# Differential attention with its probability–value products held back two blocks, six probability tiles instead of four, and GpSimd's ring of DMA descriptors at half its size

## The chip, the core and the metric

One core of one Trainium2 chip runs the whole program. The metric is the device time of one execution in microseconds (us), as the median of several; the kernel before takes 2479.04 us. Six actors are spoken of: TensorE (PE: matmuls and transposes; PEld is its weight load), VectorE (DVE), ScalarE (ACT), GpSimd (POOL, used here almost only to issue DMAs), SyncE (SP, which issues the weight loads), and the DMA engines. Each engine works through its own list of instructions in the order in which it stands, and waits where an instruction's input or buffer is not ready yet; whatever stands behind waits with it.

## What is computed

Two layers, each with three parallel token mixers (retention, differential attention, latent attention), gates, projections and a SwiGLU block, on 128 context tokens and 512 latent tokens (640 in all, five blocks of 128). Only differential attention is changed:

```python
def _diff_attention(q, k, v, lam, lam_init):
    s = jnp.einsum('bqhcd,bkhcd->bhcqk', q, k).astype(jnp.float32) * DIFF_HD ** -0.5
    p = jax.nn.softmax(s, axis=-1)
    a = p[:, :, 0] - lam * p[:, :, 1]
    o = jnp.einsum('bhqk,bkhe->bqhe', a.astype(v.dtype), v)
    return (_head_rmsnorm(o) * (1.0 - lam_init)).astype(v.dtype)
```

There are four heads; each query has two score maps (c = 0, 1), whose softmaxes are combined into one map `a` before the product with the values. Latent queries (blocks 1 to 4) see 640 keys, context queries (block 0) see 128.

## The kernel before

`diff` runs once per layer. It builds the keys, queries and values of head 0, then for each head first builds the next head (`build(hd + 1)`) and then calls `diff_head`. `diff_head` goes over the blocks in the order 1, 2, 3, 4, 0. Per block it makes, for c = 0 and 1, the scores (L836, L837, into the PSUM tile `S`, of which there are two), the maximum (L459), the exponential with its sum (L461, into an SBUF tile `dp`) and the reciprocal; the two maps are then combined in place on DVE (L850). Such a tile `dp` is taken from a group of four buffers (`bufs=4`, tag `p`).

The second half of a block, `diff_av`, is not done at once but handed to `later`, which keeps one stage back: the stage handed in before is carried out, the new one is stored. `diff_av` transposes the combined map on PE (L862, one instruction per 128 keys), ACT copies the result into `at` (L863; the one buffer of its tag), PE multiplies it with the values (L866, PSUM tile `O`, one buffer), ACT scales it into `osb` (L867) and takes the sum of squares, which writes into `at` again (L868). After the five blocks `diff_end` (also handed to `later`) makes the reciprocal root on DVE (`rsqrt`, L150 to L158, small operations in a row), scales `osb` (L875) and transposes it on PE (L880).

Between the blocks stands `self.fill()`: it takes work from a queue that `plan` laid out for this stage, 16 pieces of `gates` and 20 of `ret_values`. Both are groups of 24 matmuls each (L133) into the PSUM tile `G`, which has one buffer while filling: a gate group is emptied by ACT (L1024), a value group by ACT alone (L816) or by ACT and then DVE (L818, L819). In what follows these are called fill groups. What is left in the queue is done at the end of the stage (`flush`).

That is the order in which the program is written. The order in which each engine's list stands is set by the tile framework, which schedules the written instructions at build time; with the buffers of tag `p` it hands a free one to whichever map is next. So the written order is a priority rather than the order itself, and a number of buffers shows in it.

Retention (`ret`) follows; it needs nothing of differential attention but the memory that it leaves. On the host nothing is changed.

Of the kernel before, what the change touches and what calls it, by code (L numbers as in the profile page):

```python
# [12 lines left out]
F32 = mybir.dt.float32  # L13
# [8 lines left out]
P = 128  # L22
# [3 lines left out]
T = 640  # L26
# [24 lines left out]
class Kern:  # L51
    def __init__(self, ctx, nc, tc, io):
        self.nc, self.tc, self.io, self.ctx = nc, tc, io, ctx
        self.pe, self.act, self.dve, self.pool = nc.tensor, nc.scalar, nc.vector, nc.gpsimd

        self.pin = False
        self.gi, self.filling, self.fillers, self.pend = 0, False, [], None
        self.mod, self.ss = {}, {}
        self.const = self.sb("const", 1)
        self.hp = self.sb("hp", 1)  # L60
        self.ht = [self.hp.tile([P, KT, T], F32R, name=f"h{p}") for p in ("hi", "lo")]
        self.w = self.sb("w", 4)
        self.sm = self.sb("sm", 3)
        self.ps = ctx.enter_context(tc.tile_pool(name="ps", bufs=1, space=PSUM))
        self.dr = ctx.enter_context(tc.tile_pool(name="dr", bufs=1, space=DRAM))
# [20 lines left out]
        return self.ps.tile([P, 512], F32, tag="O", name="O", bufs=1)  # L86


    def later(self, stage):
        if self.pend is not None:  # L90
            self.pend()
        self.pend = stage


    def plan(self, points, *gens):
# [610 lines left out]
    def diff(self, l, act, yhi, ylo, ctx):  # L706
# [22 lines left out]
        def build(hd):  # L729
# [40 lines left out]
            for b0, nb in ((0, 1), (1, 2), (3, 2)):  # L770
# [9 lines left out]
                a.copy(q[:, :, 128 * b0:128 * (b0 + nb)], t.rearrange("p (c n) -> p c n", c=2)[:, :, 0:128 * nb])  # L780

        build(0)
        for hd in range(4):
            if hd < 3:
                build(hd + 1)
            self.diff_head(pool, Q[hd], K1[hd], K2[hd], V[hd], nlam, lam_init, yhi[:, hd, :], ylo[:, hd, :])
# [36 lines left out]
    def diff_head(self, pool, Q, K1, K2, V, nlam, lam_init, yhi, ylo):  # L823
        d, a, pe = self.dve, self.act, self.pe
        osb = pool.tile([P, NB, 128], F32, tag="osb", name="osb", bufs=1)
        ssq = self.sm.tile([P, NB], F32, tag="dssq", name="dssq", bufs=2)
        for b in (1, 2, 3, 4, 0):
            q0 = 128 * b
            w, nk, kb0 = (T, 5, 1) if b else (128, 1, 0)
            ps, zs = [], []  # L830
            zt = self.sm.tile([P, 8], F32, tag="dz", name="dz", bufs=4)
            for c in range(2):
                S = self.S()
                for j in range(2 if b else 1):
                    o, k0, n = (S[:, j, 0:320], 128 + 320 * j, 320) if b else (S[:, 0, 0:128], 0, 128)
                    pe.matmul(o, Q[:, c, q0:q0 + 128], K1[:, c, k0:k0 + n], start=True, stop=False)  # L836
                    pe.matmul(o, Q[:, c, q0:q0 + 128], K2[:, c, k0:k0 + n], start=False, stop=True)  # L837
                p = pool.tile([P, T], F32, tag="p", name="dp", bufs=4)
                z, tot = zt[:, c:c + 1], zt[:, c + 2:c + 3]
                if b:  # L840
                    self.softmax(S[:, :, 0:320], p.rearrange("p (a n) -> p a n", a=2), z, 0.125, tot)
                else:
                    self.softmax(S[:, 0, 0:128], p[:, :128], z, 0.125, tot)
                ps.append(p)
                zs.append((z, tot))

            r = zt[:, 4:5]
            d.scalar_tensor_tensor(r, zs[1][0], nlam, zs[0][1], op0=ALU.mult, op1=ALU.mult)
            aw = ps[0]
            d.scalar_tensor_tensor(aw[:, :w], ps[1][:, :w], r, ps[0][:, :w], op0=ALU.mult, op1=ALU.add)  # L850
            self.fill()
            self.later(lambda *x, b=b, w=w, nk=nk, kb0=kb0, aw=aw, z0=zs[0][0]: self.diff_av(pool, b, nk, kb0, aw, z0, V, osb, ssq))
        self.later(lambda: self.diff_end(pool, osb, ssq, lam_init, yhi, ylo))

    def diff_av(self, pool, b, nk, kb0, aw, z0, V, osb, ssq):
        d, a, pe = self.dve, self.act, self.pe
# [683 lines left out]


def build(arrays):
    nc = bacc.Bacc("TRN2", target_bir_lowering=False, num_devices=1)
    io = {}
    for name, a in arrays.items():
        io[name] = nc.dram_tensor(name, a.shape, mybir.dt.from_np(a.dtype), kind="ExternalInput").ap()
    for name, shape in OUTS.items():
        io[name] = nc.dram_tensor(name, shape, F32, kind="ExternalOutput").ap()
    with tile.TileContext(nc, schedule_with_timeline_sim=True) as tc, ExitStack() as ctx:
        Kern(ctx, nc, tc, io).run()  # L1550
    return nc
# [16 lines left out]
```

## Time and profile before

| | |
|---|---|
| median of three runs | 2479.04 us (2477.76 to 2480.05) |
| the profiled execution | 2480.35 us, its span on the core 2478.1 us |
| PE busy | 2399.8 us, 97% of the span |
| PEld, DVE, ACT, POOL busy | 2337.6, 1710.0, 1054.5, 155.0 us |
| DMA | 248.99 MB, mean 100 GB/s |

Read it so: PE is busy nearly all the time, and its amount of work is fixed by the program; the span is PE's work and PE's idle time. The instructions of PE overlap in the pipeline, so an instruction's duration (0.27 to 0.31 us for most) is longer than the distance to the next one. The two differential stages lie at about 320 to 494 us (layer 0) and 1549 to 1729 us (layer 1).

### The profile page before, as it was taken

The numbers are of one execution on the slowest core, as the hardware profiler recorded it, in microseconds if no ns is written. First come the engines' busy times: TensorE is split into PE (matmuls) and PEld (weight loads), VectorE is DVE, ScalarE is ACT, GpSimd is POOL, SyncE is SP. The second block draws the span as 40 slices with busy tenths as digits, with TensorE's granted clock in tenths as the row PEclk, the third lists the DMA queues.
The fourth block names the chain that finished last, engine by engine and source line by source line (L and its number), as shares of the span: only waits on it lengthen the run. The fifth ranks groups of instructions, "written<-read, shape, count | busy, mean of one in ns | idle before, by whom it ended". The sixth has DMA issues, their size and how long they took to land.

```text
span 2478.1 us, 43132 instructions
## 1 busy us (share of the span) xinstructions
PE 2399.8 (97%) x17008; PEld 2337.6 (94%) x17008; DVE 1710.0 (69%) x3835; ACT 1054.5 (43%) x2209; POOL 155.0 (6%) x266
## 2 busy tenths in 40 slices
PE   8999999999999999999999999999999999999997
PEld 5999998999999999999989999989999999999996
DVE  5767676566788766656677776765663478777776
ACT  5655565522234322222275664655322354333344
POOL 0000210000000000000000002100000000000001
PEclk9999999999999999999999999999999999999998
DMA  6211221332554444444342123213213212222222
GB/s 263 69 67 60 94 85 55 108 98 69 190 168 128 149 136 149 136 132 139 103 135 69 60 69 99 76 57 111 85 60 116 76 57 90 73 81 90 69 77 69
DMA packets 81435, 248.99 MB, mean 100 GB/s; under 512 B 10608, under 2 KB 20048, under 8 KB 80336
## 3 DMA queue, kind: packets, MB, share of 16 engines
q1 hardware_dynamic: 53856, 164.13, 20.4%
q0 software_dynamic: 21328, 76.12, 9.5%
q10 hardware_dynamic: 6048, 5.98, 0.7%
q8 instruction: 134, 2.20, 0.4%
q14 instruction: 69, 0.57, 0.1%
HBM read 225.97 MB, written 20.22 MB: 99 GB/s over the span
## 4 chain that ended last, share of the span: by engine, by line
PE 86%; DVE 7%; ACT 3%; issue 3%; DMA 1%; POOL 0%; DVEq 0%; ACTq 0%; POOLq 0%
PE G L133 35%; PE S L133 23%; PE S L1116 4%; PE S L1115 4%; PE S L1114 4%; PE Tp L133 4%; PE O L866 1%; PE Tp L669 1%; PE O L644 1%; PE O L643 1%; DVE wlo L120 1%; PE S L836 1%; PE G L217 1%; DMA rq<-dproj 1%; PE Tp L360 1%
## 5 line engine op out<-in xcount | busy, mean ns | idle before, releaser
L117 ACT CAST whi<-raw 128x1024 fp32r<-128x1024 f32 (+4 forms) x346 | 301.9, 880 | 584.3 <-PE G L133 222.3
L120 DVE TENSOR_TENSOR wlo<-raw,whi 128x1024 fp32r<-128x1024 f32 (+4 forms) x346 | 348.9, 1011 | 199.8 <-ACT whi L117 198.7
L133 PE MATMUL G<-whi,hhi 128*128 128x256 f32 x1040 | 299.1, 288 | 6.9 <-DVE rvs L819 3.9
L133 PE MATMUL G<-whi,hlo 128*128 128x256 f32 x1040 | 295.4, 284 | 0.0
L133 PE MATMUL G<-wlo,hhi 128*128 128x256 f32 x1040 | 294.4, 283 | 0.0
L1116 PE MATMUL S<-hhi,wlo 128*128 128x320 f32 x736 | 226.4, 310 | 2.6 <-DVE wlo L120 2.6
L1115 PE MATMUL S<-hlo,whi 128*128 128x320 f32 x736 | 227.5, 310 | 0.2 <-DVE hlo L120 0.2
L1114 PE MATMUL S<-hhi,whi 128*128 128x320 f32 x736 | 226.7, 309 | 0.0
L133 PE MATMUL G<-ghi,whi 128*128 128x320 f32 x704 | 220.3, 313 | 5.3 <-DVE x L1076 4.0
L133 PE MATMUL G<-glo,whi 128*128 128x320 f32 x704 | 217.4, 309 | 0.0
L133 PE MATMUL G<-ghi,wlo 128*128 128x320 f32 x704 | 217.4, 309 | 0.0
L133 PEld LDWEIGHTS G<-whi,hhi 128*128 128x128 f32 x1040 | 198.0, 191 | 10.5 <-DVE rvs L819 5.2
L133 PEld LDWEIGHTS G<-wlo,hhi 128*128 128x128 f32 x1040 | 198.4, 191 | 0.0
L133 PEld LDWEIGHTS G<-whi,hlo 128*128 128x128 f32 x1040 | 198.3, 191 | 0.0
L248 DVE SCALAR_TENSOR_TENSOR junk<-rawr,csr 128x1024 bf16<-128x1024 f32 x160 | 195.2, 1220 | 1.2
L1076 DVE SCALAR_TENSOR_TENSOR x<-G,mod,x 128x128 f32<-128x128 f32 (+2 forms) x336 | 136.3, 435 | 81.1 <-PE G L133 80.7
L133 PE MATMUL S<-hhi,whi 128*128 128x320 f32 x588 | 184.1, 313 | 2.9 <-DVE gt L1043 2.7
L133 PE MATMUL S<-hhi,wlo 128*128 128x320 f32 x588 | 181.9, 309 | 0.0
L133 PE MATMUL S<-hlo,whi 128*128 128x320 f32 x588 | 181.8, 309 | 0.0
L133 PE MATMUL G<-hhi,whi 128*128 128x320 f32 x512 | 161.7, 316 | 7.6 <-ACT gt L1024 4.7
L133 PE MATMUL G<-hlo,whi 128*128 128x320 f32 x512 | 159.1, 311 | 0.0
L133 PE MATMUL G<-hhi,wlo 128*128 128x320 f32 x512 | 158.7, 310 | 0.0
(438 smaller groups left out, 6268.6 us busy)
## 6 DMA issues: line engine op xcount, KB each, us to landing
raw<-w_ffn_in SPq DMA_DIRECT2D x88, 512.0 KB, 3.7
rawr<-w_adat POOLq DMA_DIRECT2D x80, 512.0 KB, 3.9
raw<-w_gate SPq DMA_DIRECT2D x48, 512.0 KB, 3.3
raw<-w_ffn_out SPq DMA_DIRECT2D x64, 256.0 KB, 2.7
raw<-w_diff SPq DMA_DIRECT2D x24, 512.0 KB, 3.5
raw<-w_branch SPq DMA_DIRECT2D x24, 512.0 KB, 3.6
raw<-w_ret SPq DMA_DIRECT2D x24, 512.0 KB, 3.4
raw<-w_ada SPq DMA_DIRECT2D x16, 512.0 KB, 9.7
```

Of the source, the lines that this page charges most:

```text
L117: (eng or self.act).copy(hi, src)
L120: (eng or self.dve).tensor_tensor(lo, src, hi.bitcast(F32), op=ALU.subtract)
L133: ins = self.pe.matmul(*args, **kw)
L217: self.pe.matmul(ps[32 * g:32 * g + 32, :], self.cs[:, k, :], raw[:, kk, :], start=k < 4, stop=k >= 4, tile_position=(0, 32 * g))
L248: self.tc.keep_in_program_order(d.scalar_tensor_tensor(junk, raw, 1.0, self.csr[:, i, :], op0=ALU.mult, op1=ALU.mult, accum_out=mod[:, n, ...
L360: self.pe.matmul(ps[:, :n], self.ones, sq[:, :n], start=k == 0, stop=k == KT - 1)
L643: self.pe.matmul(o[:, :n], vv, hi, start=i == 0, stop=False)
L644: self.pe.matmul(o[:, :n], vv, lo, start=False, stop=i == m - 1)
L1076: self.dve.scalar_tensor_tensor(x[h][:, n, c0:c1], ps[:, c0:c1], g[:, n, gi:gi + 1], x[h][:, n, c0:c1], op0=ALU.mult, op1=ALU.add)
L1114: self.pe.matmul(o, lh, rh, start=k == 0, stop=False)
L1115: self.pe.matmul(o, lh, rl, start=False, stop=False)
L1116: self.pe.matmul(o, ll, rh, start=False, stop=k == nk - 1)
```

## The change

`later` becomes a list: it carries out the oldest stage once more than `depth` stages are waiting. `diff_head` hands in its stages with depth 2; the latent attention calls it as before, with depth 1. The maps get six buffers. To make room, the part of each partition of SBUF that holds GpSimd's ring of DMA descriptors is set to 8192 bytes, half of the framework's default; a map tile takes 2560 bytes of a partition.

```diff
-        self.gi, self.filling, self.fillers, self.pend = 0, False, [], None
+        self.gi, self.filling, self.fillers, self.pend = 0, False, [], []
...
-    def later(self, stage):
-        if self.pend is not None:
-            self.pend()
-        self.pend = stage
+    def later(self, stage, depth=1):
+        if stage is not None:
+            self.pend.append(stage)
+        while len(self.pend) > (0 if stage is None else depth):
+            self.pend.pop(0)()
...
-                p = pool.tile([P, T], F32, tag="p", name="dp", bufs=4)
+                p = pool.tile([P, T], F32, tag="p", name="dp", bufs=6)
...
-            self.later(lambda *x, b=b, w=w, nk=nk, kb0=kb0, aw=aw, z0=zs[0][0]: self.diff_av(pool, b, nk, kb0, aw, z0, V, osb, ssq))
-        self.later(lambda: self.diff_end(pool, osb, ssq, lam_init, yhi, ylo))
+            self.later(lambda *x, b=b, w=w, nk=nk, kb0=kb0, aw=aw, z0=zs[0][0]: self.diff_av(pool, b, nk, kb0, aw, z0, V, osb, ssq), 2)
+        self.later(lambda: self.diff_end(pool, osb, ssq, lam_init, yhi, ylo), 2)
...
-    nc = bacc.Bacc("TRN2", target_bir_lowering=False, num_devices=1)
+    nc = bacc.Bacc("TRN2", target_bir_lowering=False, num_devices=1, dynamic_dma_scratch_size=8192)
```

No instruction is added or removed. What moves are places in the lists of PE, DVE, ACT and (a little) POOL, within the two differential stages and, by a few rows, at the boundary between the layers. The new `later` is one line longer, so a line after it has a number that is higher by one in the changed kernel.

**The end of layer 0's stage, PE.** These are the rows of the last head from the products of block 2 on. `O` is the product of a block, `Tp` the transposes of the next block's map `dp`, and `G_5989` is a fill group of 24 matmuls, of which the first row stands here. Before:

```order
L866 MATMUL O_5886<-V_4915,at_5876 128x128 x4
L862 MATMUL Tp_6019<-ct_76,dp_5801 128x128 x4
L866 MATMUL O_5886<-V_4915,at_5876 128x128
L862 MATMUL Tp_6025<-ct_76,dp_5801 128x128
L133 MATMUL G_5989<-whi_5921,hhi_61 128x256
...
L866 MATMUL O_6028<-V_4915,at_6018 128x128 x4
L862 MATMUL Tp_6116<-ct_76,dp_5900 128x128
L866 MATMUL O_6028<-V_4915,at_6018 128x128
L862 MATMUL Tp_6116<-ct_76,dp_5900 128x128 x3
L862 MATMUL Tp_6122<-ct_76,dp_5900 128x128
```

Of the change, the same place (block 2 is `O_6010`, block 3 `O_6107`, block 4 `O_6125`, block 0 `O_6137`):

```order
L867 MATMUL O_6010<-V_4907,at_6000 128x128 x4
L863 MATMUL Tp_6098<-ct_76,dp_5783 128x128 x4
L867 MATMUL O_6010<-V_4907,at_6000 128x128
L863 MATMUL Tp_6104<-ct_76,dp_5783 128x128
L867 MATMUL O_6107<-V_4907,at_6097 128x128 x4
L863 MATMUL Tp_6116<-ct_76,dp_5882 128x128 x4
L867 MATMUL O_6107<-V_4907,at_6097 128x128
L863 MATMUL Tp_6122<-ct_76,dp_5882 128x128
L867 MATMUL O_6125<-V_4907,at_6115 128x128 x4
L863 MATMUL Tp_6134<-ct_76,dp_6022 128x128
L867 MATMUL O_6125<-V_4907,at_6115 128x128
L867 MATMUL O_6137<-V_4907,at_6133 128x128
```

Before, a whole fill group stands between the products of block 2 and those of block 3, another behind block 3 and one behind block 4. In the change the products of blocks 2, 3, 4 and 0 stand one behind the other with only transposes between them; the fill groups that stood there have moved ahead, between the scores of this head and the one before. Behind `O_6137` come one fill group (`G_6189`) and the transposes of `diff_end`. Layer 1's stage ends in the same pattern.

**The same place, ACT.** `at` is the copy that the next products read, `osb` the scaled product. Of the change:

```order
L868 ACTIVATE osb_5501<-O_6010,dz_5620 128x128
L869 ACTIVATE at_6000,dssq_5502<-osb_5501 128x128
L864 COPY at_6097<-Tp_6098 128x512
L864 COPY at_6097<-Tp_6104 128x128
L868 ACTIVATE osb_5501<-O_6107,dz_5777 128x128
L869 ACTIVATE at_6097,dssq_5502<-osb_5501 128x128
L864 COPY at_6115<-Tp_6116 128x512
L864 COPY at_6115<-Tp_6122 128x128
```

ACT's order of these is that of before; what has moved away is the emptying of the fill groups that stood between them.

**The keys of the last head, PE.** `kh` and `kl` are the two halves of the key that are transposed into `Tp`, whose two buffers DVE and ACT empty (L761 to L763). Before:

```order
L133 MATMUL G_5427<-hhi_61,wlo_5424 128x320
L759 MATMUL Tp_4937<-identr_82,kl_4932 128x128 x2
L758 MATMUL Tp_4952<-identr_82,kh_4947 128x128 x4
L836 MATMUL S_5258<-K1_4432,Q_4491 128x320
L837 MATMUL S_5258<-K2z0_3866,Q_4491 128x320
```

Of the change (a fill group, `G_5437`, of which the first and last row stand here):

```order
L760 MATMUL Tp_4929<-identr_82,kl_4924 128x128
L134 MATMUL G_5437<-whi_5337,hhi_61 128x256
...
L134 MATMUL G_5437<-whi_5343,hlo_62 128x256
L759 MATMUL Tp_4944<-identr_82,kh_4939 128x128 x3
L760 MATMUL Tp_4945<-identr_82,kl_4940 128x128
```

Before, the transposes of the second part of the keys stand right behind those of the first part; in the change a whole fill group lies between.

## Rows read from the trace of the kernel before

**Rows 1.** The page's table of engines: busy us, share of the span, instructions.
```profile
PE 2399.8 (97%) x17008; PEld 2337.6 (94%) x17008; DVE 1710.0 (69%) x3835; ACT 1054.5 (43%) x2209; POOL 155.0 (6%) x266
```

**Rows 2.** Stretches: length, then busy time (instructions) of each engine, clock, DMA.
```profile
320.00:386.00 66.00, 63.16 (x457) 60.95 (x455) 55.57 (x154) 42.55 (x110) 9.43 (x15) 1.00 0.26 84
386.00:466.30 80.30, 76.30 (x599) 74.17 (x599) 51.83 (x151) 45.21 (x126) 3.46 (x6) 1.00 0.21 64
466.30:494.00 27.70, 25.73 (x216) 25.08 (x214) 11.42 (x39) 12.90 (x39) 2.69 (x3) 1.00 0.35 110
1549.00:1634.00 85.00, 79.29 (x578) 76.97 (x576) 64.51 (x169) 48.88 (x127) 9.66 (x15) 1.00 0.24 78
1634.00:1701.00 67.00, 63.40 (x504) 61.54 (x502) 45.85 (x140) 39.85 (x114) 3.46 (x6) 1.00 0.19 61
1701.00:1729.00 28.00, 26.03 (x219) 25.44 (x218) 11.20 (x40) 13.09 (x40) 1.08 (x2) 1.00 0.32 109
```

**Rows 3.** PE's waits in layer 0's stage: total us, times, longest.
```profile
PE Tp L758 <- DVE K2z L763: 1.4, 1, 1.4
...
PE Tp L862 <- DVE ylo L120: 1.0, 2, 0.6
PE S L836 <- ACT dp L461: 0.6, 2, 0.4
```

**Rows 4.** The same view, layer 1's stage.
```profile
PE G L133 <- ACT gt L1024: 4.2, 6, 1.2
PE S L836 <- ACT dp L461: 1.6, 5, 0.6
```

**Rows 5.** PE in time at layer 0's end: start, us, what [idle before].
```profile
472.92 1.16 PE L866 MATMUL O<-V,at 128*128 128x128 f32 x8 [0.52 <-ACT at L863]
...
474.35 0.39 PE L866 MATMUL O<-V,at 128*128 128x128 f32 x2
474.57 0.27 PE L862 MATMUL Tp<-ct,dp 128*128 128x128 f32 x1
```

**Rows 6.** ACT in time, the same place.
```profile
473.19 0.38 ACT L461 ACTIVATE dp<-S,mx 128x128 f32<-128x128 f32 x1
...
474.77 0.37 ACT L867 ACTIVATE osb<-O,dz 128x128 f32<-128x128 f32 x1 [1.11 <-PE O L866]
...
475.61 0.76 ACT L863 COPY at<-Tp 128x512 f32<-128x512 f32 x2
...
484.35 0.27 ACT L863 COPY at<-Tp 128x128 f32<-128x128 f32 x1
```

**Rows 7.** PE in time around the last product of layer 0's stage.
```profile
486.18 0.39 PE L866 MATMUL O<-V,at 128*128 128x128 f32 x2
487.63 0.38 PE L133 MATMUL G<-whi,hhi 128*128 128x256 f32 x1 [1.07 <-DVE rvs L819]
```

**Rows 8.** DVE in time: first operation of `rsqrt` and the five scalings behind it.
```profile
488.87 0.60 DVE L150 TENSOR_SCALAR rs_v<-dssq 128x5 f32<-128x5 f32 x1
...
492.70 1.16 DVE L875 TENSOR_SCALAR osb<-osb,drs 128x128 f32<-128x128 f32 x5
```

**Rows 9.** PE in time: a fill group behind one pair of scores.
```profile
459.15 0.22 PE L836 MATMUL S<-K,Q 128*128 128x128 f32 x1
...
459.78 0.39 PE L133 MATMUL G<-whi,hhi 128*128 128x256 f32 x1 [0.29 <-ACT rvs L816]
```

**Rows 10.** Stretches around the end of latent attention, columns as in Rows 2.
```profile
278.00:283.00 5.00, 3.01 (x17) 2.19 (x17) 3.34 (x7) 2.23 (x7) 4.52 (x7) 1.00 0.76 266
283.00:286.40 3.40, 3.30 (x11) 2.95 (x12) 3.10 (x5) 2.01 (x5) 1.81 (x3) 0.50 0.61 170
1511.00:1517.00 6.00, 3.91 (x21) 2.67 (x20) 4.26 (x8) 3.23 (x8) 5.26 (x9) 1.00 0.81 258
```

**Rows 11.** POOL and DVE in time: a load of queries, and its first reader.
```profile
1523.37 0.86 POOL L767 DMA_DIRECT2D rq<-dproj  x1
...
1539.53 0.43 DVE L450 TENSOR_TENSOR rp<-rq,ct 128x256 f32<-128x256 f32 x1
```

## The prediction

> **What bounds the kernel now.** I read the table of engines first: PE is busy for 97% of the span [rows 1], and the change takes none of its 17008 matmuls away. So it can act on the time only through PE's idle time inside the two differential stages. The view of stretches gives this, as length less PE's busy time [rows 2]. I cut each stage in three: the first part, to where the products of the second head begin (2.84 us idle in layer 0, 5.71 us in the longer stretch of layer 1), the middle (4.00 and 3.60 us), and the end, from the last head's products on (1.97 and 1.97 us). Together that is 20.1 us, 0.8% of the time and the most that could be won. The clock is at full rate, 1.00, in all six.
>
> Next I read who ends PE's waits. What the change aims at, a score that waits because the exponential has no free map to write into and so does not empty its `S`, is at most the waits for `dp`: 0.6 us in layer 0 [rows 3] and 1.6 us in layer 1 [rows 4], 2.2 us in all. The other waits are for something else: one of 1.4 us for DVE to empty the transposes of the keys, 1.0 us behind `diff_end`'s splits [rows 3], and in layer 1 4.2 us for ACT to empty a gate group [rows 4].
>
> **The end of each stage** is the largest term, and it is a loss. Today a fill group stands between the products of two blocks. In the change none does after block 2, so PE waits for a chain on ACT that is hidden now. Its length: the last product of block 2 starts at 474.35 and takes 0.39, so it ends at 474.74 [rows 5]; ACT starts `osb` 0.03 us later, squares, and copies the next maps from 475.61 on [rows 6]. The two copies take 0.76 together, and the shorter copy alone takes 0.27, beginning under the longer one's tail; I put the end of the first at 0.58 and the start of the next products at about 476.25, which is 1.5 us after the end of the last. PE has one transpose left to put there, until 474.84 [rows 5]. So the step from block 2 to 3 leaves 1.4 us idle, from 3 to 4 the same, and from 4 to 0, whose copy is the short one (0.27 for 0.58), 1.1. The step from 1 to 2 has five transposes and three fill matmuls over it, but both short exponentials of block 0 stand in ACT's chain now, where one stands today and PE already waits 0.52 [rows 5]; the second is 0.38 long [rows 6] and today comes behind the copy. About 0.4 more chain and 0.3 less cover: 1.2.
>
> Behind the last product comes one fill group that needs the PSUM buffer `O`, so it waits until `osb` is read: 0.5 us. Then `diff_end`'s transposes are next in PE's list. Today two fill groups stand between the last product (at 486.18, done at 486.57 [rows 7]) and them. Their chain is `osb` and square on ACT (about 0.9), then from the first operation of `rsqrt` to the first scaling 492.70 − 488.87 = 3.83 us, of which some 0.3 is a wait for DVE's earlier work, then 0.3 for the scaling [rows 8]: about 4.9 us. The wait of 0.5 and a group of 24 matmuls (24 × 0.121 = 2.9) cover 3.5 of it; 1.4 us remain, and the five scalings take 1.16 [rows 8] while five transposes need half of that, which adds 0.2: 1.6. With 0.4 us behind the first transposes, as today, the end comes to 1.2 + 1.4 + 1.4 + 1.1 + 0.5 + 1.6 + 0.4 = 7.6 us idle, against 1.97, which has the 1.07 before a fill group in it [rows 7]. That is +5.6 us per layer, **+11.2** in all. From below I take 1.0 us for each of the three steps and 0.8 for `diff_end`: +3.6 per layer; from above one more ACT operation of 0.4 in each: +7.
>
> **The middle.** The fill groups that left the end stand here. A whole one (2.9 us or more) now covers the 1.4 us wait for the keys, and another stands between `diff_end` and the next transposes, which ends the waits for `ylo` (1.0; in layer 1 about 0.5), and 0.3 of the waits for `dp` goes: −2.7, and −2.2 in layer 1, whose order here is that of layer 0. But fill groups also come to stand closer, and `G` has one buffer. Behind one pair of scores a group waits 0.29, 0.63 us after that pair began [rows 9]; two groups with nothing between (there is one such place per layer) cost that 0.63, two places with a single product or transpose between about 0.55 each, one with two transposes 0.3: +2.0. So **−0.7** and **−0.2**. Bounds: all idle there gone (−4.0, −3.6), or nothing gained and the closer groups paid (+2.0 each).
>
> **The first part.** In layer 0 PE's list hardly moves: with four buffers the scheduler already ran the scores of block 3 and 4 ahead of the products of block 1. No gain. In layer 1 the list is another one today, with 4.2 us of waits for gates and 1.6 for `dp` [rows 4]; in the change it gets the pattern that layer 0 has. Layer 0's 2.84 us, and some 0.7 for a stretch that is 19 us longer, for 5.71 [rows 2]: **−2.2**. Bounds: nothing, and −4.
>
> **The clock.** At the end of latent attention PE was busy 3.01 of 5.00 us, and for the next 3.40 us the clock stood at 0.50, the lower of its two levels (1.2 GHz); in layer 1 it was busy 3.91 of 6.00 and the clock stayed at 1.00 [rows 10]. From block 1's products to the fill group behind the last one, a new end has 5.6 us of idle time (the first five terms above) around some 5.4 us of work (four products and their transposes, 1.65 us for one block with its transposes between 472.92 and 474.57 [rows 5], less for block 0): a busy share of about 0.5, below both. If it falls for 3.4 us in one, the products there take twice as long: 1.7 us of work is lost, unless `diff_end`'s wait covers it. I take half of that, 0.8 each: **+1.6**; bounds nothing, and twice 3.4 us for each end, +6.
>
> The Trainium skill's page "TensorE: Matmul & The Clock Gate", section "A second HAM failure mode: psum-queue depth-cycling", says that short idle times between groups of matmuls can be frequent enough to switch the clock back and forth. This trace agrees for one of two places [rows 10]. By that rule both ends fall, which is the third rival below.
>
> **The ring.** Its price stands in no row, since nothing in the trace waits for it. From below it is nothing. From above, take the load of the queries that is issued last before the results' stores: its first reader comes 16 us after its issue [rows 11], so even a load that had to wait for all those ahead of it would be there. I take nothing. What covers it is that lead; without it, a late build would stop PE for the delay itself.
>
> **The sum.** 11.2 − 0.9 − 2.2 + 1.6 = +9.7 us on the profiled execution's 2480.35 us, which lies 1.3 us above the median of the runs: 2488.7 us by that median. 5 us, 0.2%, is about what a measurement of this kernel can tell from no change.
>
> **Rivals.**
> *The extra maps pay.* PE finds scores and fill work where it waits today, and the idle time outside the ends, 16.15 us [rows 2], falls to about 3 us in all. It decides once more than the ends' 11.2 us come back: 2479.0 + 11.2 − 13.1 = 2477 us, and 2474 if nothing is left of it. For it: the 1.4 us wait and those for `ylo` do get cover. Against it: the direct waits for maps are 2.2 us, and most of the rest are waits for DVE and ACT, whose work is not less. Chance 0.10.
> *The idle time only moves.* The ends cost their lower bound, +7.2, and the first part and the middle give back 5 instead of 3.1: 2481 us. For it: the amount of fill work is the same and stands elsewhere now. Chance 0.18. That the deeper list does nothing falls under this too: the first head of layer 0 shows it, where the order stays.
> *The clock falls through both ends:* 4.4 us more than I took, 2493 us. For it the low share; against it one of two places that held the clock. Chance 0.15.
> *The ring holds GpSimd back,* so that keys come late and PE waits, some 2 us for each of the six builds inside the stages, 12 us: 2500 us. Chance 0.02.
>
> **How the numbers follow.** The forecast has chance 0.55: 2488.7 us, its own range 2483 to 2493. The range that takes in the idle time that only moves, below, and the clock, above, is 2477 to 2495; it leaves out the lower half of the first rival, the fourth, and the outermost of the third and of the forecast. Slower by over 0.2% (above 2484): 0.51 of the forecast, the third and fourth, and 0.03 of the second: 0.71. Within 0.2%: the rest of the second and of the forecast and a part of the first: 0.22. Faster (below 2474 us), the first rival with ends that cost less than I say: 0.07.
>
> **What would show it.** In the changed kernel's stretches PE's idle time at the ends should be 6 to 9 us each, with PE's products (L866, now L867) waiting for ACT's `at` three to four times at 1 to 1.5 us, and `diff_end`'s transposes for DVE's `osb` over 1 us; the 1.4 us wait for the keys should be gone in both layers, and layer 1's waits for gates should fall from 4.2 to 2 us or less. The clock in the ends should show 0.5 in one or both. I am wrong if the ends show under 4 us of idle time, or if the middle falls from 4 to under 2.

## The result, and the profile after

The changed kernel takes 2499.64 us (median of six runs, 2496.86 to 2503.45), the kernel before 2478.24 us (six runs, 2477.19 to 2480.05): slower by a factor of 1.0087 (95% interval 1.0077 to 1.0097), 21.4 us. The forecast was 2488.7 us with a range to 2495: the direction was right, and the size (9.7 us) less than half of the truth. The profiled execution of the changed kernel has a span of 2498.4 us.

The table of engines of the changed kernel:

```profile
PE 2405.8 (96%) x17008; PEld 2340.8 (94%) x17008; DVE 1705.9 (68%) x3835; ACT 1054.1 (42%) x2209; POOL 155.0 (6%) x266
```

The work is the same as in [rows 1]; PE is busy for 6 us longer with the same matmuls: their durations have grown, and the rows below show a slower clock and ends that nothing overlaps. Its stretches, cut at the same instructions as [rows 2] (length, busy time of PE, PEld, DVE, ACT and POOL, clock, DMA):

```profile
320.00:386.00 66.00, 61.38 (x448) 59.81 (x446) 55.37 (x147) 42.20 (x109) 8.87 (x14) 1.00 0.25 80
386.00:481.80 95.80, 89.38 (x697) 86.24 (x698) 53.61 (x168) 48.06 (x132) 3.42 (x6) 1.00 0.21 67
481.80:505.40 23.60, 17.26 (x117) 15.86 (x116) 7.51 (x28) 9.03 (x31) 2.67 (x3) 0.86 0.33 104
1559.70:1643.90 84.20, 78.66 (x576) 76.61 (x574) 63.97 (x169) 48.43 (x125) 9.69 (x15) 1.00 0.25 79
1643.90:1725.20 81.30, 76.19 (x602) 73.52 (x602) 47.17 (x148) 43.88 (x122) 3.43 (x6) 1.00 0.20 65
1725.20:1748.00 22.80, 16.45 (x119) 15.10 (x117) 7.50 (x28) 9.29 (x32) 2.65 (x3) 0.93 0.31 94
```

Length less PE's busy time is 4.62, 6.42 and 6.34 us in layer 0 (2.84, 4.00 and 1.97 before) and 5.54, 5.11 and 6.35 us in layer 1 (5.71, 3.60 and 1.97). So the ends grew as foretold, but the middle grew too, the first part of layer 0 grew by 1.8 us, and that of layer 1 gave nothing back. In both ends the clock is below 1.00. PE's waits of the changed kernel, first for layer 0 up to its end, then for that end, then for layer 1 up to its end:

```profile
PE G L134 <- ACT gt L1025: 4.7, 6, 1.5
PE S L837 <- ACT dp L462: 4.3, 7, 1.3
...
PE O L867 <- ACT at L864: 5.1, 4, 1.4
PE G L134 <- DVE rvs L820: 1.1, 2, 0.7
PE G L134 <- ACT osb L868: 0.5, 1, 0.5
...
PE G L134 <- ACT gt L1025: 4.7, 6, 1.5
PE S L837 <- ACT dp L462: 4.3, 7, 1.3
```

The second line is the surprise. The wait of scores for the exponential, which the extra tiles were to end, was 0.6 us in layer 0 [rows 3] and 1.6 us in layer 1 [rows 4]; with six tiles it is 4.3 us in each. The 1.4 us wait for the keys is gone, as foretold; a shorter one for them (0.6 us in layer 0, 0.3 in layer 1) is left. PE in time at layer 0's end, the same place as [rows 5, 7]:

```profile
489.29 1.16 PE L867 MATMUL O<-V,at 128*128 128x128 f32 x8 [1.16 <-ACT at L864]
...
490.73 0.39 PE L867 MATMUL O<-V,at 128*128 128x128 f32 x2
490.95 0.27 PE L863 MATMUL Tp<-ct,dp 128*128 128x128 f32 x1
492.62 1.16 PE L867 MATMUL O<-V,at 128*128 128x128 f32 x8 [1.40 <-ACT at L864]
...
495.95 1.16 PE L867 MATMUL O<-V,at 128*128 128x128 f32 x8 [1.40 <-ACT at L864]
...
498.62 0.80 PE L867 MATMUL O<-V,at 128*128 128x128 f32 x2 [1.19 <-ACT at L864]
499.88 0.58 PE L134 MATMUL G<-whi,hhi 128*128 128x256 f32 x1 [0.46 <-ACT osb L868]
...
505.10 0.71 PE L881 MATMUL Tp<-ct,osb 128*128 128x128 f32 x5
```

The idle times of the five steps are 1.16, 1.40, 1.40, 1.19 and 0.46 us where the prediction had 1.2, 1.4, 1.4, 1.1 and 0.5. The last step did not come: `diff_end`'s transposes at 505.10 have no idle time before them, because the fill group ahead of them took 5.2 us instead of 2.9. The clock in these windows (1.00 is the full rate) tells why (columns as above; layer 0, then layer 1):

```profile
488.00:498.10 10.10, 5.48 (x43) 4.68 (x41) 0.90 (x4) 5.05 (x20) 0.00 (x0) 1.00 0.00 0
498.10:505.00 6.90, 5.92 (x26) 5.63 (x26) 3.90 (x21) 1.21 (x6) 2.67 (x3) 0.51 0.53 163
1733.00:1744.00 11.00, 6.56 (x51) 5.70 (x50) 0.55 (x4) 4.85 (x17) 0.90 (x1) 1.00 0.00 0
1744.00:1747.40 3.40, 3.40 (x18) 3.40 (x17) 2.92 (x18) 0.00 (x0) 1.75 (x2) 0.50 0.75 233
```

The clock fell to its lower level (1.2 GHz) at the end of both stages, behind stretches in which PE was busy 5.5 of 10.1 and 6.6 of 11.0 us. The Trainium skill's page "TensorE: Matmul & The Clock Gate", section "A second HAM failure mode: psum-queue depth-cycling", says that short idle times between groups of matmuls can be frequent enough to switch the clock back and forth. Both ends here agree; the longest idle time in them is 1.40 us.

To see where the rest came from I followed both kernels from PE instruction to PE instruction. Between 356 and 414 us PE is idle for 4.77 us in the changed kernel and for 1.65 before, 3.1 us more. ACT in time in the changed kernel's middle, somewhat later, and the PE row that waits for it:

```profile
433.62 1.05 ACT L118 CAST whi<-raw 128x1024 fp32r<-128x1024 f32 x1 [1.63 <-PE G L134]
...
434.68 0.37 ACT L868 ACTIVATE osb<-O,dz 128x128 f32<-128x128 f32 x1
...
435.07 0.31 ACT L869 ACTIVATE at<-osb 128x128 f32<-128x128 f32 x1
...
435.38 0.77 ACT L462 ACTIVATE dp<-S,mx 128x640 f32<-128x640 f32 x1
...
436.15 0.78 ACT L462 ACTIVATE dp<-S,mx 128x640 f32<-128x640 f32 x1
...
436.30 0.33 PE L837 MATMUL S<-K,Q 128*128 128x128 f32 x1 [1.07 <-ACT dp L462]
```

The first line is the split of the weights of a later fill group. It waits 1.63 us for PE to finish a group that reads the buffer it is to write, and takes 1.05; the two exponentials stand behind it on ACT, and PE's next scores wait 1.07 us for the tile `S` that they are to empty. ACT runs the exponentials with no idle time ahead of them, so they do not wait for a free map: it is ACT that is late.

### The profile page after: what moved, and what is told of

The parts are those of the page before. It is cut to its first block, busy times and chain, and to the rows that moved or that the text cites. A ratio compares the mean times of both kernels' runs of the same rounds, so it can differ in the third digit from the quotient of the medians.

```text
span 2498.4 us, 43116 instructions
## 1 busy us (share of the span) xinstructions
PE 2405.8 (96%) x17008; PEld 2340.8 (94%) x17008; DVE 1705.9 (68%) x3835; ACT 1054.1 (42%) x2209; POOL 155.0 (6%) x266
## 4 chain that ended last, share of the span: by engine, by line
PE 87%; DVE 5%; ACT 4%; issue 3%; DMA 1%; POOL 0%; DVEq 0%; ACTq 0%; POOLq 0%
PE G L134 36%; PE S L134 23%; PE S L1117 4%; PE S L1116 4%; PE S L1115 4%; PE Tp L134 4%; PE O L867 2%; PE Tp L670 1%; PE O L645 1%; PE O L644 1%; PE S L837 1%; PE S L838 1%; ACT whi L118 1%; PE G L218 1%; DVE wlo L121 1%
## 5 line engine op out<-in xcount | busy, mean ns | idle before, releaser
L134 PE MATMUL G<-whi,hhi 128*128 128x256 f32 x1040 | 301.7, 290 | 10.1 <-ACT gt L1025 4.5
```

What stands on the lines that cost most here:

```text
L134: ins = self.pe.matmul(*args, **kw)
```

## The experiments

Each run was timed beside the kernel before (2477.5 to 2477.9 us in these rounds, 2478.2 beside the change). The table sums up where each gained or lost against it, from PE's start times in the profiled executions: "layer 0" runs from the first transposes of head 0's keys (301 us before) to the first norm's sum after the mixers (L285, 781 us before), "layer 1" likewise. Outside these the profiled executions differ by up to 5 us (1519.8 us in e2, 1524.8 in the kernel before); in part the clock goes with it, which falls near 283 us or between 1511 and 1530 us in some of them and not in others, and the rest is not traced. So the medians decide, and a column tells where.

| | median us | ratio [95%] | layer 0 | layer 1 |
|---|---|---|---|---|
| the change | 2499.6 | 1.0087 [1.0077, 1.0097] | +11.6 | +11.6 |
| e1 ring only | 2478.4 | 1.0000 [0.9991, 1.0009] | −1.0 | +0.2 |
| e2 fill groups between the last products | 2485.2 | 1.0027 [1.0017, 1.0036] | +3.3 | +4.5 |
| e3 five dummies | 2505.8 | 1.0112 [1.0098, 1.0125] | +12.0 | +15.9 |
| e4 one step, six tiles | 2489.7 | 1.0045 [1.0033, 1.0058] | +4.2 | +6.1 |
| e5 two steps, four tiles | 2497.0 | 1.0077 [1.0064, 1.0090] | +8.4 | +10.8 |
| e6 splits held back | 2509.6 | 1.0126 [1.0112, 1.0140] | +15.1 | +14.9 |
| e7 before, square apart | 2470.6 | 0.9968 [0.9957, 0.9979] | −3.6 | −2.4 |
| e8 = e2, splits on GpSimd | 2495.0 | 1.0068 [1.0056, 1.0081] | +6.2 | +9.7 |
| e9 the change, square apart | 2489.1 | 1.0045 [1.0032, 1.0058] | +4.8 | +4.9 |
| e10 = e2, square apart | 2483.8 | 1.0024 [1.0013, 1.0034] | +2.8 | +4.2 |
| e11 three dummies | 2504.2 | 1.0109 [1.0095, 1.0122] | +11.8 | +15.5 |
| e12 before, two copies | 2470.2 | 0.9968 [0.9956, 0.9980] | −4.2 | −2.8 |

**e1, the ring alone.**
```diff
-    nc = bacc.Bacc("TRN2", target_bir_lowering=False, num_devices=1)
+    nc = bacc.Bacc("TRN2", target_bir_lowering=False, num_devices=1, dynamic_dma_scratch_size=8192)
```


> The kernel before with GpSimd's ring at 8192 bytes and nothing else; every engine's list is that of the kernel before, row for row. Theory A (the loss of 21 us is made by the order of the lists: the stage ends and the middle): 2478 us, within 2 us of the kernel before, and PE's gaps in both differential stages as before. Rival C (the smaller ring holds GpSimd's transfers back, rival 4 of the prediction): 2485 us or more, with PE waiting for the transposed keys or queries behind late loads. The changed kernel's first 28 us are 1.3 us shorter than before; if the ring does that, it is seen here as well.

No change, to 0.1% (the 1.0 us in layer 0 are one wait for `rvs` at 501.3 us that the profiled execution of before had and this one had not; so 1 us in a column is noise). The first 28 us are as long as before, so the 1.3 us that the changed kernel was shorter there are not the ring's. The ring's term of zero was right, and rival 4 is out.

**e2, fill groups between the last products.**
```diff
             self.diff_head(pool, Q[hd], ...)
-        self.later(None)
+        while self.pend:
+            self.fill()
+            self.pend.pop(0)()
```


> The changed kernel, but at the end of the stage a fill point stands ahead of each of the two stages that are left, so that a group of fill work stands again between the products of blocks 2, 3, 4 and 0 and two ahead of diff_end, as in the kernel before. In layer 0 PE's list is that of the changed kernel up to the third block of the last head. Theory A (ends: idle time of 6.9 us against 2.0, and the clock, 3.4 to 3.7 us more, per layer): both fall away, 8.5 us per layer, so 2499.6 - 17 = 2482.5 us (2480 to 2486); the rest of the loss, some 3 us in layer 0's middle, stays and is seen at the same rows. Rival B (the middle makes most of it, by ACT's splits of fill weights ahead of its exponentials): 2493 us or more. No clock of 0.5 in the two ends by A.

It gives 14.5 us back (2499.64 − 2485.15); by the profiled executions 8.3 us in layer 0 and 7.1 in layer 1. The clock is 1.00 through both ends. PE's waits of e2 in layer 0, up to the end and in it:

```profile
PE G L134 <- ACT gt L1027: 4.7, 6, 1.5
PE S L839 <- ACT dp L462: 4.3, 7, 1.3
...
PE O L869 <- ACT at L866: 1.2, 1, 1.2
PE G L134 <- ACT osb L870: 0.5, 1, 0.5
```

Three of the four idle steps are gone, and these two waits of the middle stand to the digit: in both layers PE's list up to the last product is that of the changed kernel, row for row, except for that list's last 28 rows. So two thirds of the loss is the ends, and 7.2 us (2485.15 − 2477.94) are the middle and the first part. The rival that gave the middle most of it is out.

**e3 and e11, the clock held up by useless matmuls.** In `diff_av`, for the last head's blocks 2, 3, 4 and 0, ahead of the products (five in e3, three in e11; nothing of the result changes; `lastv`, set in rows left out here, holds the values of the last head):
```diff
             o = self.O()
+            if V is self.lastv and b != 1:
+                for _ in range(5):
+                    pe.matmul(o[:, 256:384], self.ident, self.ident, start=True, stop=True)
...
```


> The changed kernel with five matmuls of constants (128x128, into the unused columns of O) ahead of the products of blocks 2, 3, 4 and 0 of each layer's last head, where PE is idle for 1.1 to 1.4 us; they are useless work of some 1.0 us in each idle stretch, and 40 more matmul instructions in all. If the clock's share of the ends is 3.4 us per layer, as the shift between matched rows less the idle time makes it: clock 1.00 through both ends and 2499.6 - 7 = 2493 us (2491 to 2495). If the clock costs what the prediction had in its sum (0.8 per layer): 2498 us. If the dummies are no cheaper than the idle time that they fill, or the clock falls for another reason than idle time: 2500 us or more.

> The changed kernel with three useless matmuls instead of five ahead of each of the last products, so that they end inside the idle time (five took 1.2 us and overran it by 0.1 to 0.2 us per step). Layer 0's list is that of the changed kernel up to the end of its stage, and two fill groups instead of one stand ahead of diff_end. If the clock holds and is what the end loses beside its idle time: the last product of layer 0 starts at the same distance from block 1's products as in the changed kernel, within 0.2 us, and the fill group behind it takes 2.9 and not 5.2 us. In all 2495 to 2498 us if the clock's net cost is 1 to 2 us per layer, 2500 us or more if a wait takes its place (as with five, where the second fill group waited 0.9 us for DVE).

Both totals lie in the last of my ranges, but not for the reason named there: the longer program changed the scheduled lists in layer 1's middle, and layer 1 lost some 4 us more than in the change (in e3 the clock fell there too, at 1682 us). Layer 0's list is untouched up to the end of the stage, so only that place tells something. PE in time there in e11:

```profile
489.63 1.16 PE L872 MATMUL O<-V,at 128*128 128x128 f32 x8 [0.50 <-ACT at L866]
...
491.90 0.94 PE L870 MATMUL O<-ct 128*128 128x128 f32 x6 [0.35 <-ACT osb L873]
492.95 1.16 PE L872 MATMUL O<-V,at 128*128 128x128 f32 x8
...
499.90 0.38 PE L135 MATMUL G<-whi,hhi 128*128 128x256 f32 x1 [0.46 <-ACT osb L873]
...
503.97 0.39 PE L135 MATMUL G<-whi,hhi 128*128 128x256 f32 x1 [0.93 <-DVE rvs L822]
```

The products keep their distance of 3.33 us, the dummies lie inside it, the clock stays at 1.00 and the fill group at 499.90 takes 2.9 us. From block 1's products to the first transposes of retention it is 33.6 us (486.29 to 519.93) against 34.7 in the changed kernel (485.95 to 520.68): in this end the fall of the clock costs 1.1 us net. Of the 2.3 us that it takes from the fill group a half comes back, since PE then waits only 0.4 us for DVE to empty `G`, where e11 waits 0.9 and 0.7 (in e11 a second fill group stands ahead of `diff_end`, so the two lists are not quite the same here). e3's five dummies overran the idle time by 0.1 to 0.4 us per step and gave nothing back.

**e4 and e5, one part each.**
```diff
-                p = pool.tile([P, T], F32, tag="p", name="dp", bufs=4)
+                p = pool.tile([P, T], F32, tag="p", name="dp", bufs=6)
```
is e4, to the kernel before with the halved ring. e5 is the changed kernel with this line taken back.

> The kernel before with six tiles and the halved ring, but one step deep. In its lists fill groups have moved forward too: at the end one whole group stands between blocks 2 and 3, none between 3, 4 and 0, and two groups and a bit ahead of diff_end. Theory A by its terms: two steps of 1.4 and 1.1 us idle at the end and about 0.5 at O, less what the end before had of its own (1.07 and 0.4), about +1.5 per layer and no fall of the clock (it has half of the idle time), so 2481 us if the tiles alone leave the middle as it was, and 2487 us if the tiles are what makes the middle's waits (3 us in layer 0, 2 in layer 1). Rival D (it is the second step, not the tiles, that makes all the loss): 2478 us, no change.

> The changed kernel with four tiles for the maps, as before, but two steps deep. In its lists the products of blocks 1, 2, 3, 4 and 0 of the last head all stand one behind the other (four idle steps as in the changed kernel) and two fill groups and a bit stand ahead of diff_end. The ends by the changed kernel's rows: 14.5 us, less diff_end's part, which is covered now, so +11 to +14. Theory A1 (the loss of the middle needs the extra tiles, which let scores and fill groups run ahead): the middle stays as in the kernel before, 2489 to 2492 us. Theory A2 (the second step makes the loss of the middle too): 2495 us or more, with PE's waits for dp and gt over 7 us per layer.

e4 loses 11.8 us and e5 19.1; both parts together lose 21.4, so the parts don't add up: each is another list. e4's ends have two idle steps (1.07 and 1.19 us) and a fall of the clock at layer 0's end for 3.4 us. e5's have five (6.0 us of waits for `at` per layer, 5.1 in the change) and falls in both. The waits for `dp` are 1.4 us in e5's layer 0 and 0.3 in e4's: with the square in `at`, only both parts together make them 4.3. e4 came out 3 us above the upper of my figures, because a fall of the clock and the closer fill groups (3.6 us of waits for `rvs` in layer 0) were not in it; e5 as theory A2 had it in the time, but not by the waits that A2 named (5.9 us for `dp` and `gt` together, where it wanted over 7): its loss is mostly in the ends.

**e6, the splits held back.** In `load_w`, while filling; `exps` holds the exponentials of this stage in the order of the program:
```diff
-        self.split_hi(hi, raw)
+        if self.filling and len(self.exps) >= 6:
+            with self.tc.issue_after(self.exps[-6]):
+                self.split_hi(hi, raw)
+        else:
+            self.split_hi(hi, raw)
...
```


> The changed kernel, but ACT's split of a fill group's weights (1.05 us each) may be issued at the earliest behind the exponentials of three blocks before it in the program, where the scheduler ran it up to six blocks ahead. In its lists a fill group stands again between the products of blocks 2, 3, 4 and 0 of the last head, so the ends' 14.5 us should come back whatever the middle does: 2485 us. Theory M (the 5 to 7 us that the middle and the first part lost are ACT's: splits that wait for a weight buffer stand ahead of exponentials and of the emptying of G): PE's waits for dp fall from 4.3 us per layer to under 2 and those for gt from 4.7 to under 3, and the time is 2477 to 2481 us. Rival (the lost time of the middle is ACT's and DVE's amount of work, wherever it stands): 2485 us. Rival (held splits starve the fill groups): 2490 us or more, with G waiting for whi.

The slowest of all. The ends are covered, and the waits for `gt`, 4.7 us in the change, are gone in layer 0; but those for `dp` rose to 5.5 us, and fill groups now wait for their own weights (2.7 us for `wlo`), as the last rival had it. So a split ahead of the emptying of `G` did make the gates wait, but holding it back leaves PE without fill work. Windows of e6 around the fall of the clock in layer 1's middle:

```profile
1619.00:1629.00 10.00, 7.67 (x54) 7.13 (x53) 7.42 (x19) 4.84 (x15) 1.60 (x3) 0.98 0.11 35
1629.50:1639.00 9.50, 7.81 (x27) 7.04 (x28) 6.00 (x29) 1.78 (x4) 1.14 (x2) 0.50 0.34 104
```

From the first transposes of the keys to the first of retention PE's idle times sum to 35.3 us in both layers together, those of the changed kernel to 35.6, and yet e6 is 10 us slower. Its clock is at 0.50 for 6.8, 6.8 and 10.2 us inside the stages, that of the changed kernel for 6.8 and 3.4, in the ends: 13.7 us more at half the rate, so by an estimate from these figures some 6 of the 10 us, with PE busy for most of them. The rest is not traced.

**e7 and e12, the chain through `at` freed in the kernel before.**
```diff
-            a.activation(at[:, :128], osb[:, b, :], AF.Square, accum_out=ssq[:, b:b + 1])
+            a.activation(o[:, 128:256], osb[:, b, :], AF.Square, accum_out=ssq[:, b:b + 1])
```
is e7; e12 leaves this line and takes two buffers for `at` (with the halved ring, which makes the room):
```diff
-            at = pool.tile([P, T], F32, tag="at", name="at", bufs=1)
+            at = pool.tile([P, T], F32, tag="at", name="at", bufs=2)
```


> The kernel before, with ACT's sum of squares writing its by-product into unused columns of O and not into the buffer at, so that the copy of the next maps need not wait for it; O is free some 0.5 us later. If the chain of scaled product, square and copy is what PE still waits for in the kernel before (0.5 us at the first step of an end and some of the steps in the middle): 1 to 2 us faster, 2476 to 2477 us. If O's later release is worse, or the new order of the lists brings the middle's waits as in the changed kernel: 2481 us or more. If neither is on the path: 2478 us.

> The kernel before with two buffers for the copy at (and the halved ring, which makes room and costs nothing by the first run), one step deep, four tiles, the square still writing into at. If what made the kernel with the square apart 7 us faster is that ACT's copy of the next maps no longer waits behind the square and the products that read at: the same here, 2469 to 2473 us, with PE's waits for K2z and ylo gone as there. If it was the order of the lists that happened to come out of that edit, or O's use for the square: 2475 to 2480 us.

They are 7.3 and 7.4 us faster than the kernel before, and 29 us faster than the change; I had expected 1 to 2 from e7. PE's waits in layer 0 ahead of the end, of e12:

```profile
PE G L133 <- ACT gt L1024: 3.1, 4, 1.1
PE Tp L759 <- DVE K2z L763: 0.7, 2, 0.4
```

Of the waits in [rows 3] that for the keys has fallen from 1.4 to 0.7 us, those for `ylo` are gone, and of those for `dp` 0.3 us is left. Two edits that share this, that ACT's copy of the next maps need not wait for the buffer that the products and the square hold, give the same gain. So one buffer of this chain, which the change left alone, was the tight one. It does not show in PE's own waits for `at` (0.5 us in layer 0 before, 0.6 in e12 and 1.0 in e7, with the end), but in those for the keys, `ylo` and `osb`, and in layer 1 for the gates (4.2 us before, 2.3 in e7, 3.1 in e12). Both edits also give every engine another order, and not the same one; that two orders give the same gain speaks for the buffer, but does not shut the order out.

**e8, e2 with the fill groups' splits on GpSimd.** In `load_w`, for the gates and the values (`eng` is handed down in rows left out here):
```diff
-        self.split_hi(hi, raw)
+        (eng.tensor_copy(hi, raw) if eng else self.split_hi(hi, raw))
...
```


> The kernel with fill groups between the last products (2485 us), with the splits of the fill groups' weights (128x1024) as copies on GpSimd instead of ACT: 18 splits per layer of 1.05 us leave ACT. Theory M: the waits for dp and gt in the middle fall to those of the kernel before or under, 2477 to 2481 us. Rival (ACT is not short, the groups only stand too close for the one buffer G): 2484 to 2486 us. Rival (GpSimd's copy is slow and comes late, what it costs there no run shows so far): 2487 us or more, with PE or DVE waiting for whi.

PE's waits in layer 0 ahead of the end, and GpSimd's copies there (shortest, median and longest, ns):

```profile
PE G L134 <- DVE mx L461: 2.6, 1, 2.6
PE G L134 <- DVE rvs L822: 1.5, 3, 0.8
PE G L134 <- ACT gt L1027: 1.5, 4, 0.5
```
```profile
L129 POOL CAST whi<-raw x12: 1039/1045/1766, 324.8 to 445.8; 128x1024 fp32r<-128x1024 f32 x12
```

Without the splits on ACT the waits for `dp` are gone and those for `gt` fall from 4.7 to 1.5 us: with the splits on its list ACT was late. But a new wait of 2.6 us and others came, the clock fell at 474 and 1754 us, and the kernel lost 9.8 us to e2. The copy itself is no slower than ACT's (median 1.05 us on both), but some are held up beside DVE, as the last section shows. 16 splits per layer moved, not the 18 that I had counted.

**e9 and e10, the square apart in the change and in e2** (the line of e7).

> The changed kernel with the sum of squares writing into unused columns of O, as in the run of the kernel before that came to 2470.6 us. In its lists one fill group stands between blocks 2 and 3 of the last head, none between 3, 4 and 0, and the copies for the next products no longer wait for the square. If the chain through the buffer at is the larger part of the changed kernel's loss: the ends' waits for at fall from 5.1 us per layer to under 2 and the time is 2480 us or less. If the middle's waits (dp 4.2, gt 4.7 us per layer) stay as they are: 2483 to 2487 us. If two steps and six tiles are worth something once the chain is short: under 2470.6 us.

> The changed kernel with fill groups between the last products (2485 us) and the square apart. It has both steps, six tiles and covered ends, so it tells what the second step and the extra tiles are worth against the kernel before with the square apart (2470.6 us). If they make the middle's loss whatever the chain: 2470.6 + 5 to 7 = 2476 to 2478 us. If the middle's loss comes from the chain through at: 2469 to 2472 us. Under 2469 us if they pay.

e9 gains 10.5 us on the change, as expected of a shorter chain in the ends in part only (its waits for `at` fell from 5.1 to 1.2 us per end, but the steps now wait 1.9 us for the square to leave `O`); e10 gains 1.4 on e2. Both came out above every figure that I had named. PE's waits of e9 in layer 0 up to the end:

```profile
PE G L134 <- ACT gt L1025: 4.2, 6, 1.1
...
PE S L837 <- ACT dp L462: 0.3, 1, 0.3
```

The surprise of the changed kernel, 4.3 us of waits for `dp`, is gone here (and in e10), with the splits still on ACT, both steps and six tiles: the one line of the square is enough. The waits for gates stay, and e10 gained only 1.4 us though it lost 4 us of these waits per layer: others took their place. Against e7 the two steps and six tiles cost 13 us even where the ends are covered (e10), twice what I expected. In part these are waits for `G` to be emptied: from 300 to 500 and from 1530 to 1745 us all such waits come to 7.2 and 7.7 us in e10, to 4.9 and 4.4 in e7; the rest is not traced. Two steps and six tiles are worth nothing in any form that I tried.

## Why the prediction was right or wrong

**The ends** were right in their mechanism and, partly by luck, in their sum: +11.2 and +1.6 for the clock, 12.8 us, against 14.5 measured by e2. The five idle steps came out within 0.1 us each. `diff_end`'s 1.6 did not appear as a wait: the slow clock lengthened the group that covers it, and net the clock's term (0.8 per end) measured 1.1 in layer 0. So idle time makes 4.7 us per layer of the difference to e2 where 5.6 were foretold, and PE's work, slower by the clock and less overlapped, the rest. (The terms of `diff_end`'s chain add up to 4.7 us and not 4.9, and two falls of 3.4 us in each end would cost 6.8 and not 6; neither changes the outcome.) What I left out is that a stop costs more than the idle time in the rows: between 490.73 and 492.62 the last product and the transpose behind it run out to 491.22, where in a flow the next instruction would start 0.11 us behind the transpose, at 491.06. That is 0.16 per stop, by an estimate from these rows some 0.8 per layer.

**The middle and the first part** are the step that failed: −0.9 and −2.2 foretold, +7.2 measured (e2 against before), 10 of the 12 us by which the forecast missed. By PE's idle time [rows 2] they grew by 5.5 of the 7.2 us: in layer 0 PE's waits for `G` to be emptied by 3.9 us and those for `dp` by 3.7, less 3.2 for the keys and `diff_end`; in layer 1 by 1.0 and 2.7, less 2.2. Four of the prediction's sentences fell. First, that closer fill groups cost 0.3 to 0.63 us each, +2.0 per layer: the price came from [rows 9], where ACT emptied `G` at once. With a split of 1.05 us or an exponential ahead on ACT's list it was up to 1.49, and the waits for `gt` alone came to 4.7 us per layer. Second, that layer 1 would win 2.2 us by getting layer 0's pattern: it got it, but that pattern had itself changed, and the waits for gates went from 4.2 [rows 4] to 4.7 and not to 2. Third, that the waits for `dp` would shrink: I costed the change's target by its present size and did not ask what else makes `S` late. It was ACT: these waits go when the splits leave its list (e8) and also when the splits stay and the square no longer holds `at` (e9, e10), so the splits are not their only cause. Fourth, that in layer 0's first part PE's list hardly moves: it differs from 345 us on, and the idle time there grew from 2.84 to 4.62 us. What makes all of the middle's loss is not shown: e6 moved the splits in time, e8 to another engine and e10 the square, each took away at least one of the two large waits, and each lost elsewhere. The waits for `ylo` and the long one for the keys did go, as foretold.

**The clock** fell in both ends, as rival 3 had it (2493 us, 0.15), but its net price, where it could be read (1.1 us in layer 0's end), was near what the forecast took; the time beyond 2493 came from the middle. **The ring** cost nothing (e1). **Rivals 1 and 2** (the tiles pay, the idle time only moves) are out: idle time outside the ends grew from 16.15 to 21.69 us. Of the signs that I named for being right those of the ends, the keys and the clock came; `diff_end`'s wait and the fall of layer 1's waits for gates did not. The ends had over 4 us of idle time, and the middle grew, so neither of the signs that I named for being wrong came; I had named none for a middle that loses.

## What to carry to other kernels

A deeper pipeline or more buffers of one kind help only if that buffer is what the waiting engine waits for; look for what holds it (here ACT's list, and the one buffer `at`: a second one gave 7.4 us, two more maps cost 11.8 and, with a second step, 21). Under a scheduler a buffer count is an edit to every engine's list, so fill work that covers a tail may be used up earlier: count what is left for the stage's end, and put it there by hand as in e2. Price a wait by what stands ahead of the releasing operation on its own engine, not by a row where nothing did.

## What the runs showed of the hardware that was not expected

The same list with the same idle times kept the clock in some executions and lost it in another. These are windows of the changed kernel and of e11, whose lists agree here row for row on PE, ACT, DVE and POOL:

```profile
429.50:438.50 9.00, 6.11 (x47) 5.49 (x46) 5.26 (x17) 6.84 (x15) 1.81 (x3) 1.00 0.40 114
438.50:441.70 3.20, 2.74 (x23) 2.54 (x22) 2.93 (x13) 0.37 (x1) 1.61 (x3) 1.00 1.01 227
```
```profile
429.00:438.00 9.00, 6.10 (x45) 5.48 (x45) 5.77 (x20) 6.56 (x14) 2.46 (x5) 0.98 0.45 144
438.30:441.50 3.20, 2.74 (x14) 2.44 (x14) 2.93 (x14) 0.37 (x1) 0.67 (x2) 0.57 0.89 243
```

PE was busy 6.1 of 9.0 us in both, with the same three idle times (1.49, 1.07 and 0.34 us), and only in e11 did the clock fall behind it. e2 and e3 have the same lists and the same idle times here too, and kept the clock. So in these runs such a stretch is a chance of a fall, one in four, and not a certain price.

The other is what DVE and GpSimd do to each other. In e8 a copy on GpSimd (128x1024) overlapped DVE's subtraction of two SBUF operands (`wlo`, the same size) five times. Two of them:

```profile
324.80 1.04 POOL L129 CAST whi<-raw 128x1024 fp32r<-128x1024 f32 x1 [7.28 <-issue]
324.88 2.04 DVE L121 TENSOR_TENSOR wlo<-raw,whi 128x1024 fp32r<-128x1024 f32 x1
```
```profile
445.45 1.23 DVE L121 TENSOR_TENSOR wlo<-raw,whi 128x1024 fp32r<-128x1024 f32 x1 [1.00 <-POOL whi L129]
445.81 1.77 POOL L129 CAST whi<-raw 128x1024 fp32r<-128x1024 f32 x1 [0.40 <-PE G L134]
```

In all five the one that began first took its usual time (1.04 us on GpSimd, 1.22 on DVE), and the one that began second was longer: 1.46 to 1.77 us on GpSimd, 1.75 and 2.04 on DVE. The Trainium skill's page "GPSIMD Engine Reference", section "1. Specifications", says that GpSimd shares its way to SBUF with VectorE when that reads two operands from there, and this agrees.
